# Attention scores as three passes of split operands, one sum untied, last products in halves

## The chip, the cores and the metric

The kernel runs on one core of a Trainium2 chip. The core has a matrix engine (TensorE, PE in the profile, with PEld for its weight loads), a vector engine (VectorE, DVE), a scalar engine (ScalarE, ACT), a general engine (GpSimd, POOL) and a queue engine that issues transfers (SyncE, SP). Each works through its own instructions in order; semaphores tie them together. The metric is the device time of one execution in microseconds. The kernel before takes 1212.84 us, the median of three runs from 1212.77 to 1212.94.

## The reference

A trunk of two layers over one sequence of 256 tokens with 1024 features, all float32. Each layer is a half-step feed-forward block, a mixer and another half-step feed-forward block, each followed by a layer norm of `alpha * x + h`:

```python
for l in range(DEPTH):
    h = _swiglu(x, ffn_w1[l, 0], ffn_w3[l, 0], ffn_w2[l, 0])
    x = _layernorm(ALPHA * x + 0.5 * h, ln_g[l, 0], ln_b[l, 0])
    h = _mixer(x, l, w_in[l], ...)
    x = _layernorm(ALPHA * x + h, ln_g[l, 1], ln_b[l, 1])
    h = _swiglu(x, ffn_w1[l, 1], ffn_w3[l, 1], ffn_w2[l, 1])
    x = _layernorm(ALPHA * x + 0.5 * h, ln_g[l, 2], ln_b[l, 2])
```

The mixer projects x to seven parts: u and v for a gating unit with causal mixing of positions, q, k and values for attention, and two gates. The attention has 8 heads, and each head has two halves of 64 dimensions with a softmax of their own:

```python
q, k = _rope(q, cos, sin), _rope(k, cos, sin)
s = jnp.einsum('bqhmd,bkhmd->bhmqk', q_blk, k) * scale     # m: the two halves of a head
p = jax.nn.softmax(jnp.where(mask, s, neg), axis=-1)
a = p[:, :, 0] - lam * p[:, :, 1]
o = jnp.einsum('bhqk,bkhe->bqhe', a, v)
```

Queries are taken in blocks of 128, so the first block sees 128 keys and the second 256.

## The kernel before, in words

**Split operands.** The large products are made from float32 values that are split in two: a high part, rounded to the type F32R by a copy on ACT, and a low part, the difference, by a subtraction on DVE. A product is then three multiplies of F32R: high by high, high by low, low by high. `split` (L232) does this for activations, `stream` (L155) for weights: a transfer into `raw`, a copy on ACT (L174) to `whi`, a subtraction on DVE (L178) to `wlo`. `three` (L268) issues the three multiplies for row-wise products; `gemm_a2` (L273) does column-wise products for two blocks of 128 output features, with 16 multiplies of 512 columns from the high weights (L283) and 16 of 256 from the low weights (L290).

**Order.** TensorE's instructions run in the order in which the program issues them. For the other engines a planner chooses the order from priorities; `soon()` raises the priority, and `behind(ins)` places an instruction after `ins` in its engine's order. Work that belongs beside the weight products, such as attention, is written as generators: `beside(task, delay)` starts one after a delay, and each `yield w` lets `w` units pass. Time for them is counted in `beat`s of the issued products; one call of `gemm_a2` for one weight block is two units. So delays decide where in TensorE's order a task's multiplies stand.

**Attention.** For each of four pairs of heads, `rope` (L795) makes q and then k with `gemm_a2`, exchanges rows by four transfers on SyncE's queue (L801), multiplies by the cosine on DVE (L804) and the sine on GpSimd (L805), and `rest` adds the two (L809), 1.55 units later (1.25 for the last). It returns one float32 tile of 128 rows by 512 columns: the rows are the two halves `m` of a head, 64 each, and the columns are two heads `j` of 256 tokens. `attend` (L815) starts 3.9 units after k. `exps(1)` (256 keys) and, 0.6 units later, `exps(0)` (128 keys) each issue four score calls at L829, for two heads and two halves, plain float32, 64 rows high, into one bank of TensorE's accumulators (PSUM) per half. DVE then adds the mask and takes the row extreme (L837), ACT takes the exponentials (L839), DVE combines the halves (L848), TensorE transposes (L863, L868), ACT copies (L865, L870), TensorE multiplies by the values (L876, L878), and ACT copies and squares that sum (L881, L886). The banks for this come from four `side` banks in turn; the four `main` banks serve the projections.

**Norms.** Each norm adds bank sums to the residual rows, for two blocks of 128 rows (t) and two halves of 512 columns (c): `part_s` (L542) on DVE, with a row sum. `finish_s` (L548) makes the mean (L551), squares on ACT (L553), an inverse root by short DVE steps, and the normalised rows (L556). Then `turn` (L622) brings the rows into the transposed layout, by TensorE transposes (L633) or transfers, and splits them (L233, L234) for the next stage. `xlo[0, 0]` is the subtraction that ends the first of these for t = 0. In the mixer `done` (L996) issues both sums of a row block at the end of its products, after the first rows' `turn`; in the feed-forward block the sums are issued half by half (L767).

**The end.** The last norm works with `part` (L562): a sum, statistics by groups of 256 columns and, for the last rows, a product with the gain (L574), which the finish (L576) uses: TensorE forms parts of the result from it (L588, L592) while DVE computes the inverse root. For the last rows and columns 512 to 1023 the loop at L761 issues 24 multiplies of 512 columns into one bank and then handles two halves of 256.

Of the kernel before, what the change touches and what calls it, by code (L numbers as in the profile page):

```python
# [11 lines left out]
F32 = mybir.dt.float32  # L12
# [8 lines left out]
P = 128  # L21
D = 1024
T = 256
# [35 lines left out]
def trunk(ctx, tc, x, xT, w13a, w13b, w2s, w2p, wb, wqk, wa, wbr, wo, gateb, sgug, sgub, sguwT, sgubias, lam, diffg,  # L59
# [91 lines left out]
    def behind(ins):  # L151

        return tc.issue_after(ins) if ins is not None else nullcontext()
# [355 lines left out]
    class Norm:  # L509
# [31 lines left out]

        def part_s(self, t, c, ps, scale=1.0):  # L542
            y = self.y[t][:, c * 512 : (c + 1) * 512]
            with behind(self.xlo.get((0, 0))):
                V.scalar_tensor_tensor(out=y, in0=y, scalar=scale, in1=ps, op0=ALU.mult, op1=ALU.add,
                                       accum_out=self.st[t][:, c : c + 1])

# [103 lines left out]
    def ffn(l, f, i, norm, following=None):  # L651
# [108 lines left out]
            ln.pre = ahead(following)  # L760
        for t in range(NT):  # L761
            for c in range(2):
                for ps, o, n in ends[t, c]:
                    for q in PQ[-HELD:]:
                        rows_p(ps, t, q, held[q, c], hh, hl, o, n, stop=q == PQ[-1])
                    if not last:
                        ln.part_s(t, c, ps)  # L767
                        continue
                    for o in ((0, 256) if last and (t, c) == (1, 1) else (0,)):
                        ln.part(t, c * 512 + o, ps[:, o : o + 256] if o or last and (t, c) == (1, 1) else ps, 1.0)  # L770
            (ln.finish if last else ln.finish_s)(t, ((2, 1.5), (2, 1))[t])
            if t == 0:
                with behind(ln.ends[0]):
                    ln.more(1, 0, S[7], ALU.subtract, ln.scale)
                    ln.more(1, 0, u, ALU.add)
                    ln.more(1, 1, v, ALU.add, ln.scale)
                    ln.more(1, 1, S[7], ALU.add)
        return ln.close()

    def mixer(l, i, norm):  # L780
# [14 lines left out]
        def rope(src, scale, last=False):  # L795

            (_, z), = gemm_a2([src], both, lambda m: slots("z", 2)[0], lambda: t512("r"), scale)
            sw, r = t512("swap"), slots("qk", 2)[0]
            for q in range(4):
                o, i = q * 32, (q ^ 1) * 32  # L800
                nc.sync.dma_start(sw[o : o + 32, :], z[i : i + 32, :])  # L801
            r3, z3, s3 = (v.rearrange("p (j t) -> p j t", j=2) for v in (r, z, sw))
            c, s = (v.unsqueeze(1).to_broadcast([P, 2, T]) for v in (cos_t, sin_t))
            V.tensor_tensor(out=r3, in0=z3, in1=c, op=ALU.mult)  # L804
            turned_by[0] = G.tensor_tensor(out=s3, in0=s3, in1=s, op=ALU.mult).ins  # L805

            def rest():
                with behind(None if last else added[0]):
                    V.tensor_tensor(out=r, in0=r, in1=sw, op=ALU.add)  # L809
                yield 0  # L810

            beside(rest(), 1.25 if last else 1.55)
            return r

        def attend(hp, qT, kT):  # L815
            mx, sums = sm("mx", 8), sm("sums", 8)
            c4 = sm("c", 4)
            rc = sm("rc", 4)

            def rows(z, m, j, o, n):  # L820
                return z[m * HD : (m + 1) * HD, j * T + o : j * T + o + n]

            def exps(t):

                nk = (t + 1) * P
                banks = [side_bank() for _ in range(2)]
                for j in range(2):
                    for m in range(2):
                        PE.matmul(banks[m][:, j * nk : (j + 1) * nk], rows(qT, m, j, t * P, P), rows(kT, m, j, 0, nk),  # L829
                                  start=True, stop=True)  # L830
                pp = []
                for m in range(2):
                    o = m * 4 + t * 2
                    p = s512("pp")[:, : 2 * nk]
                    for j in range(2):
                        s, a = slice(j * nk, (j + 1) * nk), slice(o + j, o + j + 1)
                        V.tensor_tensor_reduce(out=p[:, s], in0=banks[m][:, s], in1=mask[:, T - nk :], scale=-1.0,  # L837
                                               scalar=BIG, op0=ALU.add, op1=ALU.min, accum_out=mx[:, a])
                        A.activation(p[:, s], p[:, s], AF.Exp, bias=mx[:, a], scale=-1.0, accum_out=sums[:, a])  # L839
                    pp.append(p)  # L840
                return pp

            def less(t, pp):

                nk = (t + 1) * P
                for j in range(2):
                    s = slice(j * nk, (j + 1) * nk)
                    V.scalar_tensor_tensor(out=pp[0][:, s], in0=pp[1][:, s], scalar=c4[:, t * 2 + j : t * 2 + j + 1],  # L848
                                            in1=pp[0][:, s], op0=ALU.mult, op1=ALU.add)
                return pp[0]  # L850

            second = exps(1)
            yield 0.6
            first = exps(0)
            V.reciprocal(out=rc, in_=sums[:, 4:])
            V.scalar_tensor_tensor(out=c4, in0=rc, scalar=neg_lam[l], in1=sums[:, :4], op0=ALU.mult, op1=ALU.mult)
            second, first = less(1, second), less(0, first)
            yield 2.6
            b = side_bank()
            for j in range(2):  # L860
                for c in range(2):
                    o = (j * 2 + c) * P
                    PE.transpose(b[:, o : o + P], second[:, o : o + P], ident)  # L863
            aT1 = slots("aT", 2)[0]
            A.activation(aT1, b, AF.Copy)  # L865
            b = side_bank()
            for j in range(2):
                PE.transpose(b[:, j * P : (j + 1) * P], first[:, j * P : (j + 1) * P], ident)  # L868
            aT0 = slots("aT", 2)[0][:, :T]
            A.activation(aT0, b[:, :T], AF.Copy)  # L870
            yield 2.3
            b = side_bank()
            for j in range(2):
                h = hp * 2 + j
                v = [val[c][:, h // 4, (h % 4) * P : (h % 4 + 1) * P] for c in range(2)]
                PE.matmul(b[:, j * P : (j + 1) * P], aT0[:, j * P : (j + 1) * P], v[0], start=True, stop=True)  # L876
                for c in range(2):
                    PE.matmul(b[:, T + j * P : T + (j + 1) * P], aT1[:, (j * 2 + c) * P : (j * 2 + c + 1) * P],  # L878
                               v[c], start=c == 0, stop=c == 1)
            on = slots("on", 2)[0]  # L880
            A.activation(on, b, AF.Copy)  # L881
            ss, s2 = sm("ss", 4), sm("s2", 4)
            A.activation(s2, sums[:, :4], AF.Square, scale=(2 * HD * EPS) ** 0.5)
            for q in range(4):
                s = slice(q * P, (q + 1) * P)
                A.activation(b[:, s], b[:, s], AF.Square, accum_out=ss[:, q : q + 1])  # L886
            yield 2
            with behind(turned_by[0]):
                G.tensor_tensor(out=ss, in0=s2, in1=ss, op=ALU.add)
            r = rsqrt4(ss, 1.0 / (2 * HD))  # L890
            yield 2
            both_ = tmp.tile([P, 2, 512], F32, tag="columns", name=name("both"), bufs=1)
            os, pk = both_[:, 0], both_[:, 1].bitcast(U16)
            for q in range(4):
                t, j = q // 2, q % 2
                with behind(emptied[0]):
                    A.activation(os[:, j * T + t * P : j * T + (t + 1) * P], on[:, q * P : (q + 1) * P], AF.Copy,
                                 scale=r[:, q : q + 1])
            planes(pk, os)
            tt = turning(pk, 4)  # L900
            yield LAND
            b = slots("turned", 2)[0]
            join(b, tt)
            dl = dgs[:, l : l + 1]
            for j in range(2):
                h, s = hb[hp * 2 + j], slice(j * T, (j + 1) * T)
                A.activation(h[:, :T], b[:, s], AF.Copy, scale=dl)
                V.scalar_tensor_tensor(out=h[:, T:], in0=b[:, s], scalar=dl, in1=h[:, :T].bitcast(F32),
                                        op0=ALU.mult, op1=ALU.subtract)

        for hp in range(HEADS // 2):
            qT = rope(wqk[l, hp, 0], HD ** -0.5)
            kT = rope(wqk[l, hp, 1], 1.0, hp == HEADS // 2 - 1)
            beside(attend(hp, qT, kT), 3.9)

        gates = []
        for br, sec in ((0, GA_), (1, GB_)):
# [183 lines left out]
```

## Time and profile before

| | us |
|---|---|
| median of the runs | 1212.84 |
| lowest, highest | 1212.77, 1212.94 |
| the profiled execution | 1213.05 |
| its span | 1211.3 |
| TensorE busy | 1203.7 (99%) |
| VectorE busy | 942.9 (78%) |
| ScalarE busy | 857.4 (71%) |
| GpSimd busy | 91.1 (8%) |

The span runs from the first to the last profiled instruction; the device time has 1.75 us around it. Names like L829 are lines of the kernel. In a timeline a row is a start, a length and a group of like instructions, with their count after the x; several rows may overlap, since multiplies are pipelined and their ends are modelled. In brackets stands how long the engine was idle before the row and whose work ended that. A row of windows gives, for one stretch, its length and then the busy time and count of TensorE, its weight loads, VectorE, ScalarE and GpSimd, the granted clock, the share of the transfer engines and GB/s. A row of groups gives the count, the total and the mean time (ns) and the idle time before.

### The profile page before, as it was taken

The numbers are of one execution on the slowest core, as the hardware profiler recorded it, in microseconds if no ns is written. First come the engines' busy times: TensorE is split into PE (matmuls) and PEld (weight loads), VectorE is DVE, ScalarE is ACT, GpSimd is POOL, SyncE is SP. The second block draws the span as 40 slices with busy tenths as digits, with TensorE's granted clock in tenths as the row PEclk, the third lists the DMA queues.
The fourth block names the chain that finished last, engine by engine and source line by source line (L and its number), as shares of the span: only waits on it lengthen the run. The fifth ranks groups of instructions, "written<-read, shape, count | busy, mean of one in ns | idle before, by whom it ended". The sixth has DMA issues, their size and how long they took to land.

```text
span 1211.3 us, 16542 instructions
## 1 busy us (share of the span) xinstructions
PE 1203.7 (99%) x5961; PEld 1011.3 (83%) x5961; DVE 942.9 (78%) x1540; ACT 857.4 (71%) x1384; POOL 91.1 (8%) x184
## 2 busy tenths in 40 slices
PE   9999999999999999999999999999999999999998
PEld 8888888888888878888888888888888888888886
DVE  6658998885696876579985679989766877757797
ACT  7677677679865595776776776776898556867761
POOL 0100000233300000000000000003331000000000
PEclk9999999999999999999999999999999999999999
DMA  8985665655764658665668665766648456677551
GB/s 321 323 261 174 211 249 208 227 177 166 232 227 164 217 178 282 191 192 218 229 216 270 195 176 207 254 223 199 213 139 273 176 174 217 201 259 210 184 202 47
DMA packets 101346, 257.00 MB, mean 212 GB/s; under 512 B 66528, under 2 KB 67600, under 8 KB 74640
## 3 DMA queue, kind: packets, MB, share of 16 engines
q1 hardware_dynamic: 97296, 243.03, 59.9%
q0 software_dynamic: 3536, 12.13, 3.2%
q8 instruction: 46, 0.75, 0.3%
q10 hardware_dynamic: 432, 0.79, 0.2%
q14 instruction: 36, 0.29, 0.1%
HBM read 235.47 MB, written 1.05 MB: 195 GB/s over the span
## 4 chain that ended last, share of the span: by engine, by line
PE 91%; DVE 4%; ACT 3%; issue 1%; DMA 0%; SPq 0%; POOL 0%; DVEq 0%; ACTq 0%; POOLq 0%
PE bank L271 35%; PE sbank L271 24%; PE bank L283 16%; PE bank L290 8%; PE sbank L283 2%; PE bank L446 2%; PE sbank L290 1%; PE sbank L829 1%; DVE wlo L178 1%; PE sbank L961 1%; ACT pp L839 0%; DVE nwa L248 0%; ACT xf L638 0%; ACT whi L174 0%; PE sbank L878 0%
## 5 line engine op out<-in xcount | busy, mean ns | idle before, releaser
L178 DVE TENSOR_TENSOR wlo<-raw,whi 128x1024 fp32r<-128x1024 f32 (+1 forms) x396 | 436.6, 1125 | 144.5 <-ACT whi L174 113.9
L174 ACT ACTIVATE whi<-raw 128x1024 fp32r<-128x1024 f32 (+1 forms) x396 | 372.9, 971 | 124.4 <-PE bank L283 43.2
L271 PE MATMUL bank<-whi,x 128*128 128x512 f32 x840 | 263.3, 390 | 0.0
L271 PEld LDWEIGHTS bank<-whi,x 128*128 128x128 f32 x840 | 157.7, 188 | 32.9 <-DVE gz L293 0.2
L271 PE MATMUL bank<-wlo,x 128*128 128x512 f32 x420 | 163.5, 389 | 0.0
L271 PE MATMUL sbank<-whi,x 128*128 128x512 f32 x512 | 158.9, 389 | 0.0
L283 PE MATMUL bank<-x,whi 128*128 128x512 f32 x640 | 156.0, 394 | 0.0
L283 PEld LDWEIGHTS bank<-x,whi 128*128 128x128 f32 x640 | 117.1, 188 | 26.3 <-issue 2.3
L271 PEld LDWEIGHTS sbank<-whi,x 128*128 128x128 f32 x512 | 96.1, 188 | 20.0
L353 ACT ACTIVATE shi<-raw 128x1024 fp32r<-128x1024 f32 (+1 forms) x80 | 73.4, 946 | 51.7 <-DVE raw L368 26.4
L271 PE MATMUL sbank<-wlo,x 128*128 128x512 f32 x256 | 99.6, 389 | 0.0
L355 DVE TENSOR_TENSOR slo<-raw,shi 128x1024 fp32r<-128x1024 f32 (+1 forms) x80 | 85.4, 1088 | 14.1 <-ACT shi L353 13.3
L271 PEld LDWEIGHTS bank<-wlo,x 128*128 128x128 f32 x420 | 78.9, 188 | 16.0
L290 PE MATMUL bank<-x,wlo 128*128 128x256 f32 x640 | 85.9, 285 | 0.0
L290 PEld LDWEIGHTS bank<-x,wlo 128*128 128x128 f32 x640 | 81.6, 191 | 2.2
L291 ACT ACTIVATE r<-bank 128x256 f32<-128x256 f32 x112 | 41.6, 377 | 24.0 <-PE bank L290 24.0
L271 PEld LDWEIGHTS sbank<-wlo,x 128*128 128x128 f32 x256 | 48.1, 188 | 9.9
L271 PE MATMUL sbank<-whi,hhi 128*128 128x512 f32 x144 | 56.3, 391 | 0.0
L271 PE MATMUL sbank<-whi,hlo 128*128 128x512 f32 x144 | 56.1, 390 | 0.0
L271 PE MATMUL sbank<-wlo,hhi 128*128 128x512 f32 x144 | 56.0, 389 | 0.0
L506 POOL DMA_DIRECT2D bc<-in_lng x6 | 3.2, 530 | 696.2 <-DVE bc L505 696.2
L702 ACT ACTIVATE planes<-silu 128x1024 uint16<-128x1024 uint16 x40 | 42.0, 1053 | 7.3 <-DVE silu L701 6.2
(247 smaller groups left out, 1999.1 us busy)
## 6 DMA issues: line engine op xcount, KB each, us to landing
raw<-in_w13b SPq DMA_DIRECT2D x76, 1024.0 KB, 5.4
raw<-in_w2p SPq DMA_DIRECT2D x24, 1024.0 KB, 4.9
raw<-in_wa SPq DMA_DIRECT2D x24, 1024.0 KB, 5.4
raw<-in_w2s SPq DMA_DIRECT2D x20, 1024.0 KB, 4.9
raw<-in_wb SPq DMA_DIRECT2D x16, 1024.0 KB, 5.3
raw<-in_wqk SPq DMA_DIRECT2D x16, 1024.0 KB, 4.8
raw<-in_wbr SPq DMA_DIRECT2D x16, 1024.0 KB, 4.9
raw<-in_w13a SPq DMA_DIRECT2D x8, 1024.0 KB, 4.8
```

The costliest lines, as they stand in the source:

```text
L174: copied = A.activation(h, r, AF.Copy)
L178: V.tensor_tensor(out=w, in0=r, in1=h.bitcast(F32), op=ALU.subtract)
L271: PE.matmul(ps, xx, w, start=start and n == 0, stop=stop and n == 2)
L283: PE.matmul(b[-1], hi[:, k * P : (k + 1) * P], xc(k), start=k == 0, stop=False)
L290: PE.matmul(b[n][:, :T], lo[:, k * P : (k + 1) * P], xc(k)[:, :T], start=False, stop=k == KT - 1)
L291: emptied[0] = A.activation(r[:, s], b[n][:, T:], AF.Copy, scale=scale).ins
L353: A.activation(h, r, AF.Copy)
L355: V.tensor_tensor(out=w, in0=r, in1=h.bitcast(F32), op=ALU.subtract)
L446: PE.matmul(ps[t][m], x[:, j, o + t * P : o + (t + 1) * P], y, start=k0 + j == 0 and o == 0 and y is hi, stop=k0 + j == KT - 1 and y is lo)
L702: A.activation(pk.rearrange("p (w k) -> p w k", w=2), s.bitcast(U16).rearrange("p (k w) -> p w k", w=2), AF.Copy)
L829: PE.matmul(banks[m][:, j * nk : (j + 1) * nk], rows(qT, m, j, t * P, P), rows(kT, m, j, 0, nk), start=True, stop=True)
L961: PE.matmul(b[:, j * T + t * P : j * T + (t + 1) * P], vg[t][:, g // 4, s], wsT[g // 4][:, s], start=True, stop=True)
```

## The change

Three edits.

1. `rope` now returns two F32R tiles: a copy of the sum r on ACT, issued with raised priority, and 0.5 units later a subtraction on DVE for the low part. The score calls become three per head and half, (q high, k high), (q high, k low), (q low, k high), which add up in the same bank; the loop over the two halves is innermost. `attend` starts 4.4 units after k in place of 3.9. Each rope takes two more tiles of the pool.
2. `part_s` places only the second half's sum (c = 1) behind `xlo[0, 0]`; the first half's sum has no such place.
3. For the last rows and the last 512 columns, the multiplies are issued as 24 of 256 columns into the left half of the old bank and 24 into a new bank. The left half is finished (sum, statistics, product with the gain) when its multiplies are done, and what the old bank's right half holds from earlier products is added to the rows by one more DVE sum.

```diff
         def part_s(self, t, c, ps, scale=1.0):
             y = self.y[t][:, c * 512 : (c + 1) * 512]
-            with behind(self.xlo.get((0, 0))):
+            with behind(self.xlo.get((0, 0)) if c else None):
                 V.scalar_tensor_tensor(out=y, in0=y, scalar=scale, in1=ps, op0=ALU.mult, op1=ALU.add,
                                        accum_out=self.st[t][:, c : c + 1])
...
         for t in range(NT):
             for c in range(2):
-                for ps, o, n in ends[t, c]:
-                    for q in PQ[-HELD:]:
-                        rows_p(ps, t, q, held[q, c], hh, hl, o, n, stop=q == PQ[-1])
-                    if not last:
-                        ln.part_s(t, c, ps)
-                        continue
-                    for o in ((0, 256) if last and (t, c) == (1, 1) else (0,)):
-                        ln.part(t, c * 512 + o, ps[:, o : o + 256] if o or last and (t, c) == (1, 1) else ps, 1.0)
+                (ps, _, _), = ends[t, c]
+                if last and (t, c) == (1, 1):
+                    y, right = ln.y[t][:, 768:], bank()
+                    for b, o, opens in ((ps, 0, False), (right, 256, True)):
+                        for q in PQ[-HELD:]:
+                            rows_p(b[:, :T], t, q, held[q, c], hh, hl, o, 256, stop=q == PQ[-1],
+                                   start=opens and q == PQ[-HELD])
+                        ln.part(t, 512 + o, b[:, :T], 1.0)
+                        if not opens:
+                            V.tensor_tensor(out=y, in0=y, in1=ps[:, T:], op=ALU.add)
+                    continue
+                for q in PQ[-HELD:]:
+                    rows_p(ps, t, q, held[q, c], hh, hl, 0, 512, stop=q == PQ[-1])
+                if last:
+                    ln.part(t, c * 512, ps, 1.0)
+                else:
+                    ln.part_s(t, c, ps)
...
-            sw, r = t512("swap"), slots("qk", 2)[0]
+            sw, r, hi = t512("swap"), slots("qk", 2)[0], slots("qkh", 4, F32R)
...
             def rest():
                 with behind(None if last else added[0]):
                     V.tensor_tensor(out=r, in0=r, in1=sw, op=ALU.add)
-                yield 0
+                with soon():
+                    A.activation(hi[0], r, AF.Copy)
+                yield 0.5
+                with behind(None if last else added[0]):
+                    V.tensor_tensor(out=hi[1], in0=r, in1=hi[0].bitcast(F32), op=ALU.subtract)
 
             beside(rest(), 1.25 if last else 1.55)
-            return r
+            return hi
...
                 for j in range(2):
-                    for m in range(2):
-                        PE.matmul(banks[m][:, j * nk : (j + 1) * nk], rows(qT, m, j, t * P, P), rows(kT, m, j, 0, nk),
-                                  start=True, stop=True)
+                    for n, (q, k) in enumerate(((0, 0), (0, 1), (1, 0))):
+                        for m in range(2):
+                            PE.matmul(banks[m][:, j * nk : (j + 1) * nk], rows(qT[q], m, j, t * P, P),
+                                      rows(kT[k], m, j, 0, nk), start=n == 0, stop=n == 2)
...
-            beside(attend(hp, qT, kT), 3.9)
+            beside(attend(hp, qT, kT), 4.4)
```

## The prediction

> **What bounds the kernel now.** I read the page first: busy times, then the chain that ended last.
>
> ```profile
> span 1211.3 us, 16542 instructions
> PE 1203.7 (99%) x5961; PEld 1011.3 (83%) x5961; DVE 942.9 (78%) x1540; ACT 857.4 (71%) x1384; POOL 91.1 (8%) x184
> PEclk9999999999999999999999999999999999999999
> PE 91%; DVE 4%; ACT 3%; issue 1%; DMA 0%; SPq 0%; POOL 0%; DVEq 0%; ACTq 0%; POOLq 0%
> L290 PEld LDWEIGHTS bank<-x,wlo 128*128 128x128 f32 x640 | 81.6, 191 | 2.2
> ```
>
> TensorE is busy 99% of the span at full clock and carries 91% of the chain. The loads of the low weights, L290, wait for no producer worth naming: weights are split long before use. A microsecond counts, then, only if it is taken out of TensorE's own stream, out of a place where that stream stands, or out of the tail. The chain of waits in order of time gives the steps of that stream, and timelines of single stretches give the rest.
>
> ```profile
> 209.16 1.91 PE bank L290 x16
> 211.08 3.65 PE bank L283 x16
> ...
> 27.70 21.76 PE sbank L271 x96
> ```
>
> A split multiply of 512 columns steps by 21.76/96 = 0.227 us, one of 256 columns by 1.91/16 = 0.119 us.
>
> **Edit 1: the scores.** Timelines of TensorE: one head pair of the second layer, the last head pair of the first layer, and transposes.
>
> ```profile
> 841.34 1.13 PE L829 MATMUL sbank<-qk,qk 64*128 64x256 f32 x8
> 842.40 2.14 PE L283 MATMUL bank<-x,whi 128*128 128x512 f32 x8
> 844.47 0.72 PE L829 MATMUL sbank<-qk,qk 64*128 64x128 f32 x8
> 845.11 1.19 PE L283 MATMUL bank<-x,whi 128*128 128x512 f32 x4
> ...
> 272.22 1.94 PE L829 MATMUL sbank<-qk,qk 64*128 64x256 f32 x8
> 274.08 0.96 PE L283 MATMUL bank<-x,whi 128*128 128x512 f32 x3
> ...
> 273.02 0.73 PEld L829 LDWEIGHTS sbank<-qk,qk 64*128 64x128 f32 x6 [0.51 <-ACT sbank L886]
> ...
> 269.57 0.60 PE L863 MATMUL sbank<-ident,pp 128*128 128x128 f32 x4
> 270.00 0.38 PE L868 MATMUL sbank<-ident,pp 128*128 128x128 f32 x2
> ```
>
> Each head pair has two blocks: 256 keys, 842.40 - 841.34 = 1.06 us, and 128 keys, 845.11 - 844.47 = 0.64 us. A block is four calls and shows eight records, so a plain f32 call is two records. Eight records in 0.64 us are 0.08 us each, while one full-height multiply of 128 columns steps by 0.43/4 = 0.1075 us (the transposes). So the two 64-row halves run side by side: a block is four slots of two records. The blocks differ by 0.42 us over four slots: 0.105 us per slot and 128 columns. What stays, 1.06 - 8 x 0.105 = 0.22 us, is the block's entry and exit.
>
> After the change each call is three split calls, each one record, halves alternating: six slots per block. With 256 keys a slot is between 0.105 (half of the present 0.21) and 0.119 (L290); I take the middle, 0.112: 0.22 + 6 x 0.112 = 0.89, a gain of 0.17. With 128 keys no row shows a split multiply. Below: half of today's slot, 0.0525, makes 0.535, a gain of 0.10. Above: twice today's slot, 0.21, makes 1.48, a loss of 0.84. The nearest row is the transpose, one record, same columns, same weight load: 0.1075, so 0.22 + 0.645 = 0.865, a loss of 0.225. Together +0.055 us per head pair, **+0.4 us** over eight (ends -2.5 and +5.7). Six slots replace four: where a load of 128 columns sets the pace, halving the passes gains nothing.
>
> The Trainium skill, page "TensorE: Matmul & The Clock Gate", section LDWEIGHTS, speaks against this edit: a load's time goes with its columns, not its rows, some 107 ns for 128; its section on weight-path modes adds that the fast load is not for FP32. By that rule the short block comes out as taken above, and the transpose step of 0.1075 us agrees. The page "FP8 and Floating Point Precision", section TensorE Precision Notes, counts true FP32 as four passes; three for four by columns alone would shorten both blocks, the first rival below.
>
> The split itself adds one ACT copy and one DVE subtraction of 128x512 per rope, 16 of each (groups of the page and of the view by line, a window over six ropes, and two rows of DVE in it):
>
> ```profile
> L178 DVE TENSOR_TENSOR wlo<-raw,whi 128x1024 fp32r<-128x1024 f32 (+1 forms) x396 | 436.6, 1125 | 144.5 <-ACT whi L174 113.9
> L174 ACT ACTIVATE whi<-raw 128x1024 fp32r<-128x1024 f32 (+1 forms) x396 | 372.9, 971 | 124.4 <-PE bank L283 43.2
> ...
> L233 ACT ACTIVATE hhi<-columns 128x512 fp32r<-128x512 f32 x20 | 12.5, 623 | 0.0
> L234 DVE TENSOR_TENSOR hlo<-columns,hhi 128x512 fp32r<-128x512 f32 x20 | 13.8, 689 | 3.5 <-ACT hhi L233 3.1
> ...
> 227.00:272.00 45.00, 45.00 (x288) 38.06 (x287) 38.29 (x102) 34.31 (x100) 13.24 (x21) 1.00 0.59 199
> ...
> 268.78 0.61 DVE L848 SCALAR_TENSOR_TENSOR pp<-pp,c,pp 128x128 f32<-128x128 f32 x2
> 269.31 0.68 DVE L809 TENSOR_TENSOR qk<-qk,swap 128x512 f32<-128x512 f32 x1
> ```
>
> In that window DVE is busy 38.3 of 45 us and ACT 34.3; six ropes add 6 x 0.69 = 4.1 to the one, 94%, and 6 x 0.62 = 3.7 to the other, 85%. Neither becomes the bound, and the weights keep their lead; that is the cover. Behind the copy on ACT stand exponentials and weight copies, behind the subtraction on DVE the lows and row sums. The tight places are the attention's own steps. In the first layer the last pair's block stood 0.51 us for a bank that ACT L886 still read, and the break in alternation cost more: 1.86 against 1.06. One copy of 0.62 us ahead of L886 makes that 0.6 longer. Transposes at 270.00 follow their input (269.39) by 0.6 us, and a copy and a subtraction (1.31) could eat that: I take 0.2 in each layer. **+1.0 us** in all; below, -0.8 (the half unit by which attention moves lets the bank come free), above the fourth rival. The half unit itself costs TensorE nothing: the same multiplies are dealt out later, with the projections filling in.
>
> **Edit 2: the sum at the mixers' norms.** Timeline around the first mixer's end, and the transposes that waited:
>
> ```profile
> 423.39 0.69 DVE L178 TENSOR_TENSOR wlo<-raw,whi 128x512 fp32r<-128x512 f32 x1
> ...
> 426.12 0.69 DVE L234 TENSOR_TENSOR x<-xf,x 128x512 fp32r<-128x512 f32 x1 [2.05 <-ACT x L233]
> 426.73 0.68 DVE L545 SCALAR_TENSOR_TENSOR xtok<-xtok,bank 128x512 f32<-128x512 f32 x1
> 427.52 0.63 ACT L174 ACTIVATE whi<-raw 128x512 fp32r<-128x512 f32 x1
> 428.04 0.63 ACT L233 ACTIVATE x<-xf 128x512 fp32r<-128x512 f32 x1
> 428.06 0.21 DVE L551 TENSOR_SCALAR mv<-st 128x1 f32<-128x1 f32 x1
> 428.56 1.14 ACT L553 ACTIVATE sq<-xtok,mv 128x1024 bf16<-128x1024 f32 x1
> ...
> 425.90 0.39 PE L271 MATMUL bank<-whi,mlo 128*128 128x512 f32 x1
> ...
> 433.11 0.39 PE L271 MATMUL bank<-whi,x 128*128 128x512 f32 x1
> 433.89 0.66 PE L633 MATMUL sbank<-ident,xtok 128*128 128x128 f32 x4 [0.39 <-DVE xtok L556]
> ```
>
> DVE stands 2.05 us before L234. The first bank's last multiply is 12 before the one at 425.90, at 423.18, so its sum fits in the idle time, and the second sum and the mean come 0.6 us earlier (the sum's place at 426.73 is free). The goal would be the transposes' stand, 433.89 - 433.11 - 0.227 = 0.55 us, once per mixer. But the squares (L553) start when ACT has finished L233, not when the mean is there: 428.06 + 0.21 = 428.27 against 428.56. A mean at 427.67 finds ACT just begun on L174 (427.52), and only another order on ACT turns it into time. **0** taken, nearest to that row; ends -1.1 (both stands gone) and 0: the idle 2.05 us excludes a loss. At the feed-forward norms nothing is tied yet when the first sum of the second rows is issued, so nothing moves.
>
> **Edit 3: the last products.** Timeline of the end:
>
> ```profile
> 1197.48 0.39 PE L271 MATMUL sbank<-whi,hhi 128*128 128x512 f32 x1
> ...
> 1200.05 0.69 DVE L574 TENSOR_TENSOR xtok<-xtok,bc 128x512 f32<-128x512 f32 x1
> ...
> 1202.69 0.40 PE L271 MATMUL sbank<-whi,hlo 128*128 128x512 f32 x1
> 1203.13 0.75 DVE L567 TENSOR_TENSOR xtok<-xtok,sbank 128x256 f32<-128x256 f32 x2 [2.38 <-PE sbank L271]
> 1204.46 0.41 DVE L574 TENSOR_TENSOR xtok<-xtok,bc 128x256 f32<-128x256 f32 x1
> 1204.78 0.26 DVE L579 BATCH_NORM_AGGREGATE mv<-st 128x2 f32<-128x24 f32 x1
> ```
>
> Now 24 multiplies of 512 from 1197.48, the sum 0.44 after the last start, and 1.65 us of two sums, two statistics and a product until the aggregate. Then 48 of 256: the last starts at 1197.48 + 47 x 0.119 = 1203.07, its sum 0.44 - 0.108 later (the shorter multiply), 1203.40, which is 0.27 late; but only one sum and one statistic are left, 0.42 each with 0.04 behind: aggregate at 1204.32, **-0.45 us**, and everything after it waits for it in order. The left half's four operations (the added sum among them, 1.84 us) start at 1200.74, when L574 is done, and end at 1202.6: hidden by the right half's multiplies with 0.8 to spare; uncovered, the added sum costs 0.42. Ends: -0.7 (step 0.1135, half of 0.227) and 0.
>
> **Sum:** 0.4 + 1.0 + 0 - 0.45 = +0.95. The profiled execution took 1213.05 us for its span of 1211.3, 0.2 above the median 1212.84, so 1214.0 for it and **1213.8** for the median.
>
> **Rivals.** (a) *Columns set the pace, not loads.* Slots 0.105 and 0.0525: -0.21 and -0.105 per pair, x 8 = -2.5; with -0.45 and no new waits 1209.9. For it: halves load at the same time today. Against: no record of 128 columns steps under 0.105. (b) *Short split multiplies run at a quarter rate*, slots 0.21: (0.84 - 0.17) x 8 = +5.4, with 0.55 from the rest 1218.8. For: the kernel has no split multiply under 256 columns. Against: nothing in the trace slows with fewer columns. (c) *Halves do not overlap in split form*: 12 steps, 1.65 and 1.51 us, +1.46 x 8 = 11.7: 1225.1. Against: the f32 halves overlap, and their order alternates. (d) *The split comes late.* The last k was summed at 269.99, its block began at 272.22: 2.2 us; half a unit (1.4 us, a rope of 5.57 us being two units) makes 3.6. Copy, subtraction, one ACT weight copy and one DVE low ahead of them (0.62 + 0.69 + 0.97 + 1.13 = 3.4) use it up. From a second weight copy on, TensorE stands 1.0 at each of the four later pairs: +4.2 with 0.4 - 0.45 gives 1217.0. (e) *Edit 2 does nothing*, because ACT keeps its order: that is the forecast.
>
> **Chances.** Forecast 0.53 with its own range 1212.0 to 1215.8; (a) 0.18; (b) 0.10; (c) 0.05; (d) 0.14. The range 1210.0 to 1218.0 leaves out (c), most of (b) and the outer side of (a). Within 0.2% (2.4 us) is what I call no change: faster 0.16 ((a) but for its inner edge, and a little of the forecast), slower 0.30 ((b), (c), (d)), same 0.54.
>
> **What would show it.** Blocks of L829's successor at 0.89 and 0.865 us with 12 records in six slots: step right; 0.535 for the short one: (a); above 1.4: (b) or, with starts not in pairs, (c). Waits of score loads for the subtraction: (d). The squares still starting behind L233: edit 2 as forecast. The aggregate 1.25 us behind the last multiply's start: edit 3. Wrong would be a total outside 1212.0 to 1215.8, or within it by cancelling errors.

## The result

The changed kernel takes 1226.43 us (median of 4 runs, 1225.79 to 1227.10), the kernel before 1212.80 us on the same chip (1212.56 to 1212.94). The ratio is 1.0114, with a 95% interval of 1.0101 to 1.0126. That is 13.6 us slower, outside the predicted range of 1210 to 1218. The profiled execution took 1225.79 us.

From the page of the changed kernel: span, TensorE's and the other engines' busy time, and the shares of the chain that ended last.

```profile
span 1224.1 us, 16754 instructions
PE 1208.5 (99%) x6049; PEld 1018.0 (83%) x6049; DVE 950.6 (78%) x1557; ACT 864.9 (71%) x1400; POOL 85.8 (7%) x184
...
PE 87%; DVE 5%; ACT 3%; DMA 1%; POOL 1%; issue 1%; SPq 1%; DVEq 0%; POOLq 0%; ACTq 0%
```

TensorE is busy 4.8 us more, in a span that is 12.8 us longer: it now stands for 15.6 us instead of 7.6. POOL, SP's queue and the DMA, which had 0% of the chain, have 1% each. A landmark tells where: the transposes that wait at the second rows of each mixer's norm, before (first row, the second layer; the first layer's stands in the prediction, at 433.89) and after.

```profile
1032.84 0.55 PE L633 MATMUL sbank<-ident,xtok 128*128 128x128 f32 x3 [0.38 <-DVE xtok L556]
```

```profile
439.69 0.66 PE L633 MATMUL sbank<-ident,xtok 128*128 128x128 f32 x4 [0.29 <-DVE xtok L556]
...
1046.01 0.66 PE L633 MATMUL sbank<-ident,xtok 128*128 128x128 f32 x4 [0.33 <-DVE xtok L556]
```

The first layer loses 439.69 - 433.89 = 5.8 us, the second 1046.01 - 1032.84 - 5.8 = 7.4, and the rest gains 13.2 - 12.8 = 0.4. TensorE's timeline of the changed kernel shows an ordinary head pair, and the last head pair of each layer:

```profile
229.63 0.97 PE L843 MATMUL sbank<-qkh,qkh 64*128 64x256 f32 x12
230.53 2.14 PE L283 MATMUL bank<-x,whi 128*128 128x512 f32 x8
232.60 0.89 PE L843 MATMUL sbank<-qkh,qkh 64*128 64x128 f32 x12
233.41 0.86 PE L290 MATMUL bank<-x,wlo 128*128 128x256 f32 x5
...
274.45 0.38 PE L843 MATMUL sbank<-qkh,qkh 64*128 64x256 f32 x1
279.11 1.65 PE L843 MATMUL sbank<-qkh,qkh 64*128 64x256 f32 x11 [4.28 <-ACT aT L879]
...
884.42 1.65 PE L843 MATMUL sbank<-qkh,qkh 64*128 64x256 f32 x11 [4.19 <-ACT aT L879]
886.00 3.78 PE L283 MATMUL bank<-x,whi 128*128 128x512 f32 x8
```

The score blocks themselves are near the forecast: 230.53 - 229.63 = 0.90 us and 233.41 - 232.60 = 0.81 us. But in the last pair of each layer the second half of the first block stands 4.28 and 4.19 us for a side bank from which ACT has not yet copied the transposes of the pair before. Behind it the clock falls: eight multiplies that take 2.14 us in the ordinary pair (230.53) take 3.78. By stages of the changed kernel (the columns end with the granted clock, the DMA share and GB/s):

```profile
272.00:281.00 9.00, 4.72 (x28) 3.67 (x26) 3.67 (x8) 8.46 (x24) 0.43 (x2) 0.90 0.56 157
281.00:284.00 3.00, 3.00 (x16) 2.16 (x15) 1.05 (x8) 3.00 (x11) 1.93 (x10) 0.74 0.84 317
877.00:884.00 7.00, 3.23 (x19) 2.40 (x17) 2.52 (x5) 6.14 (x14) 0.74 (x2) 0.95 0.62 183
884.00:891.00 7.00, 6.58 (x33) 5.06 (x34) 2.71 (x10) 6.53 (x22) 3.07 (x15) 0.56 0.48 155
```

Length of the stage times the missing share of the clock is what the clock costs: 9 x 0.10 + 3 x 0.26 = 1.7 us in the first layer and 7 x 0.05 + 7 x 0.44 = 3.4 in the second. With the stands that is 6.0 and 7.6, against 5.8 and 7.4 lost. So two stands, and the clock behind them, account for the loss, to 0.2 us in each layer.

Why the bank is late is read backwards. First ACT in the changed kernel, ahead of that copy:

```profile
260.34 0.63 ACT L820 ACTIVATE qkh<-qk 128x512 fp32r<-128x512 f32 x1 [2.94 <-DVE qk L818]
...
272.54 0.99 ACT L911 ACTIVATE both<-on,nwy 128x128 f32<-128x128 f32 x3 [3.57 <-POOL nwy L264]
...
278.00 0.58 ACT L895 ACTIVATE on<-sbank 128x512 f32<-128x512 f32 x1
278.47 0.58 ACT L879 ACTIVATE aT<-sbank 128x512 f32<-128x512 f32 x1
```

ACT stands 3.57 us in front of the scaling of the first pair's output (L911), and the copy (L879) is some 6 us behind it in the same queue. The scaling waits for the inverse root of the first pair, which is on GpSimd. GpSimd's timeline before, and after:

```profile
259.69 0.20 POOL L889 TENSOR_TENSOR ss<-s,ss 128x4 f32<-128x4 f32 x1
...
265.44 0.20 POOL L264 TENSOR_TENSOR nwy<-nwa,nwy 128x4 f32<-128x4 f32 x1
265.62 1.30 POOL L805 TENSOR_TENSOR swap<-swap,sin_t 128x512 f32<-128x512 f32 x1
```

```profile
264.20 1.30 POOL L814 TENSOR_TENSOR swap<-swap,sin_t 128x512 f32<-128x512 f32 x1 [4.62 <-DMA swap<-z]
265.47 0.19 POOL L903 TENSOR_TENSOR ss<-s,ss 128x4 f32<-128x4 f32 x1
...
270.91 1.32 POOL L263 TENSOR_SCALAR nwa<-nwa 128x4 f32<-128x4 f32 x1
272.31 0.20 POOL L264 TENSOR_TENSOR nwy<-nwa,nwy 128x4 f32<-128x4 f32 x1
```

Before, the root ran from 259.69 to 265.64, ahead of the eighth rope multiply. After, the half unit by which attention starts later has put the root behind that multiply, and the multiply waits 4.62 us for the exchange of the last k's rows by DMA. The root ends at 272.51: 6.9 us later, of which 5.8 are its later start and 1.1 its own greater length.

### The profile page after: what moved, and what is told of

Same layout as the page of the kernel before. It is cut to its first block, busy times and chain, and to the rows that moved or that the text cites. A ratio compares the mean times of both kernels' runs of the same rounds, so it can differ in the third digit from the quotient of the medians.

```text
span 1224.1 us, 16754 instructions
## 1 busy us (share of the span) xinstructions
PE 1208.5 (99%) x6049; PEld 1018.0 (83%) x6049; DVE 950.6 (78%) x1557; ACT 864.9 (71%) x1400; POOL 85.8 (7%) x184
## 4 chain that ended last, share of the span: by engine, by line
PE 87%; DVE 5%; ACT 3%; DMA 1%; POOL 1%; issue 1%; SPq 1%; DVEq 0%; POOLq 0%; ACTq 0%
PE bank L271 35%; PE sbank L271 23%; PE bank L283 14%; PE bank L290 8%; PE sbank L283 2%; PE bank L446 2%; PE sbank L290 1%; DMA swap<-z 1%; DVE wlo L178 1%; SPq L810 1%; PE sbank L843 1%; ACT whi L174 1%; PE sbank L975 1%; DVE nwa L248 0%; POOL swap L814 0%
## 5 line engine op out<-in xcount | busy, mean ns | idle before, releaser
L178 DVE TENSOR_TENSOR wlo<-raw,whi 128x1024 fp32r<-128x1024 f32 (+1 forms) x396 | 434.9, 1120 | 170.5 <-ACT whi L174 138.8
L283 PE MATMUL bank<-x,whi 128*128 128x512 f32 x640 | 160.4, 400 | 0.0
L271 PE MATMUL sbank<-whi,hhi 128*128 128x512 f32 (+1 forms) x144 | 55.5, 386 | 0.0
L271 PE MATMUL sbank<-whi,hlo 128*128 128x512 f32 (+1 forms) x144 | 55.3, 384 | 0.0
L271 PE MATMUL sbank<-wlo,hhi 128*128 128x512 f32 (+1 forms) x144 | 55.2, 384 | 0.0
```

Source lines behind the costliest of these rows:

```text
L178: V.tensor_tensor(out=w, in0=r, in1=h.bitcast(F32), op=ALU.subtract)
L271: PE.matmul(ps, xx, w, start=start and n == 0, stop=stop and n == 2)
L283: PE.matmul(b[-1], hi[:, k * P : (k + 1) * P], xc(k), start=k == 0, stop=False)
```

## The experiments

Two theories stood at the start. *Order*: the later start puts the first pair's root behind the eighth rope multiply on GpSimd, and that makes the bank late. *Queues*: the copy and the subtraction, standing ahead of other work in the in-order queues of ACT and DVE, make it late. Some expectations call these A and B.

**late_only**: the kernel before with the later start alone.

```
-            beside(attend(hp, qT, kT), 3.9)
+            beside(attend(hp, qT, kT), 4.4)
```

> The kernel before with one number changed: attention starts 4.4 units after k in place of 3.9; scores stay plain f32, nothing is split. Theory A (order): the later start alone puts the first pair's inverse root on GpSimd behind the last rope's multiply, ACT stands for it, and the last pair's score block waits over 4 us for a bank in each layer: 1219 to 1227, the first eight inverse-root steps on GpSimd only after the eighth rope multiply. Theory B (split work): the copies on ACT and subtractions on DVE make the queues late; without them 1212 to 1214.

Measured: 1218.46 us (1216.75 to 1219.41), ratio 1.0046 (1.0031 to 1.0061). Timelines of late_only:

```profile
276.25 1.13 PE L829 MATMUL sbank<-qk,qk 64*128 64x256 f32 x6 [1.83 <-ACT aT L865]
...
261.08 1.54 POOL L805 TENSOR_TENSOR swap<-swap,sin_t 128x512 f32<-128x512 f32 x1 [1.79 <-DMA swap<-z]
...
269.68 0.70 ACT L897 ACTIVATE both<-on,nwy 128x128 f32<-128x128 f32 x2 [4.35 <-POOL nwy L264]
```

The same stand at the same bank, without any split, by the same path; it is shorter, 1.83 us for 4.28, and here the eighth multiply starts at 261.08, not 264.20. The later start alone costs 5.8 us (the kernel before took 1212.70 in the same rounds), a little under half of the loss.

**split_early**: the changed kernel with the start as before.

```
-            beside(attend(hp, qT, kT), 4.4)
+            beside(attend(hp, qT, kT), 3.9)
```

> The changed kernel with attention started 3.9 units after k as before; split, sum and last products as changed. Theory A: GpSimd's order is that of before, so no wait of 4 us; what is left is the split's own cost of 0 to 2 us: 1211.5 to 1214.5. Theory B: the copies and subtractions are all there and have less time, so at least as slow as the changed kernel: 1225 or more.

Measured: 1226.37 us (1225.42 to 1227.79), 1.0114 (1.0098 to 1.0129): no gain, so order alone is not the answer. Timelines of split_early, GpSimd, DVE and TensorE:

```profile
263.01 1.30 POOL L814 TENSOR_TENSOR swap<-swap,sin_t 128x512 f32<-128x512 f32 x1 [12.75 <-DMA swap<-z]
269.42 1.28 POOL L814 TENSOR_TENSOR swap<-swap,sin_t 128x512 f32<-128x512 f32 x1
...
270.74 0.69 DVE L818 TENSOR_TENSOR qk<-qk,swap 128x512 f32<-128x512 f32 x1 [3.66 <-POOL swap L814]
...
273.36 0.84 PE L877 MATMUL sbank<-ident,pp 128*128 128x128 f32 x4 [2.84 <-DVE pp L862]
```

Here the root is ahead of the eighth multiply again, as before the change. But the seventh multiply, behind which the root stands, starts at 263.01 and not at 258.43 as before the change, so root and eighth multiply are late, and with them the last k's sum on DVE; the third pair's weighted differences (L862) stand behind that sum, and the transposes wait for them. In addition the waits of TensorE show 1.5 us for k's low half (L823) in four blocks.

**tail_as_before**: the changed kernel with an earlier place for the transposes, so that the steps behind them fall where they fell before.

```
-            yield 2.6
+            yield 2.1
```

> The changed kernel with the transposes' delay 2.1 in place of 2.6 units, so that all of attention behind the scores is issued where it was before, while the scores start later. Theory A: 1211.5 to 1214.5, with the inverse root of the first pair between the seventh and the eighth rope multiply on GpSimd. Theory B: 1224 to 1227, the last pair's block held by 4 us or more.

Measured: 1216.13 us (1215.38 to 1217.12), 1.0030 (1.0019 to 1.0041). On GpSimd the root stands ahead of the eighth multiply. The first blocks of pairs 2 and 3 still run 0.55, 0.58, 0.55 and 0.79 us over 0.90, for a side bank. Three quarters of the loss is gone, and neither theory had this number.

**sum_and_halves**: edits 2 and 3 alone; the diff is that of the change without its attention hunks.

> Only the untied sum and the last products in halves, scores as before. Prediction: the aggregate of the last norm 0.45 us earlier, the squares of the mixers' norms where they were: 1212.2 to 1212.5. If the squares do move and the transposes no longer stand, 1211.2 to 1211.8.

Measured: 1212.23 us (1212.02 to 1212.79), 0.9996 (0.9987 to 1.0006), as expected: no measurable difference.

**root_early**: the changed kernel, with the root half a unit earlier and the rest where it was.

```
             for q in range(4):
                 s = slice(q * P, (q + 1) * P)
                 A.activation(b[:, s], b[:, s], AF.Square, accum_out=ss[:, q : q + 1])
-            yield 2
+            yield 1.3
             with behind(turned_by[0]):
                 G.tensor_tensor(out=ss, in0=s2, in1=ss, op=ALU.add)
             r = rsqrt4(ss, 1.0 / (2 * HD))
-            yield 2
+            yield 2.7
```

> The changed kernel with one step of the attention moved: the yield ahead of a head pair's inverse root is 1.3 instead of 2, the next one 2.7 instead of 2. TensorE's order of work stays that of the changed kernel; on GpSimd the first pair's inverse root goes back ahead of the eighth rope multiply, as before the change. Theory order (the eighth rope multiply ahead of the first root on GpSimd is what makes scaling, aT copies and so the bank late): last pairs' S1 blocks lose their 4.2 us stands, the clock stays near 1 behind them, 1214 to 1218 us. Theory queues (the copy and the subtraction, standing ahead of other work in the in-order queues of ACT and DVE, are what makes it late, whatever GpSimd's order): the stands stay above 2 us, 1221 to 1227 us.

Measured: 1220.95 us (1220.57 to 1221.57), 1.0066 (1.0051 to 1.0081). TensorE's instructions and their order are the changed kernel's; what moves is the root on GpSimd, back ahead of the eighth multiply, and the time falls by 5.5 us. The root is not the only thing that moves: behind it ACT and DVE have another order too (ACT's L895 is at 272.52, ahead of two weight copies, where the changed kernel has it at 278.00 behind them). So the 5.5 us belong to the root's place together with the order that follows from it. The time lies between what the two theories gave. The rest is again a stand at the last pairs' first blocks, but for another reader of a bank. Timeline of root_early:

```profile
880.03 1.19 PE L843 MATMUL sbank<-qkh,qkh 64*128 64x256 f32 x11 [2.29 <-ACT sbank L900]
881.16 3.43 PE L283 MATMUL bank<-x,whi 128*128 128x512 f32 x8
```

Now it is the bank of the last products, held until ACT has done four squares (L900) between weight copies.

**nosoon**: the changed kernel without the raised priority of the copy.

```
-                with soon():
-                    A.activation(hi[0], r, AF.Copy)
+                A.activation(hi[0], r, AF.Copy)
```

> The changed kernel without the raised priority of the copy on ACT: the copy of a rope's high half then stands in ACT's queue where its issue puts it. GpSimd's order is that of the changed kernel. Theory order: no gain, 1224 to 1228 us, with stands near 4 us at the last pairs' S1 blocks. Theory queues, in the form that the copy standing 2.9 us ahead of the first pair's aT copies makes those late: the stands fall below 2.5 us, as in late_only, and the time to 1217 to 1221 us.

Measured: 1226.09 us (1225.25 to 1226.76), 1.0107 (1.0090 to 1.0124). But the edit moved nothing: ACT's instructions come in the same order as in the changed kernel, and the stand ahead of the copy (260.34 above) is still there. Timeline of nosoon:

```profile
260.47 0.63 ACT L819 ACTIVATE qkh<-qk 128x512 fp32r<-128x512 f32 x1 [2.93 <-DVE qk L818]
```

So this run says nothing for or against the queues.

**keep_nosoon**: both of the above, the transposes' place of tail_as_before and no raised priority.

> The changed kernel with the yield ahead of the transposes 2.1 instead of 2.6 (as tail_as_before, 1216.1 us) and without the raised priority of the copy on ACT; GpSimd's order is that of before the change. Theory order: the same as tail_as_before, 1215.5 to 1217 us. Theory queues: another gain, 1213 to 1215 us. Should the score loads then wait for a late high half, 1217 to 1221 us, with waits for ACT's copy at the S1 blocks.

Measured: 1216.08 us (1215.69 to 1216.85), 1.0028 (1.0017 to 1.0039), the same as tail_as_before. Here too ACT's order is that of the run without the edit, so this is tail_as_before once more and no test.

**copies_unused** and **a39_copies_unused**: copies and subtractions made, scores in f32 from the unsplit q and k; the start at 4.4 and at 3.9.

```
-                    for n, (q, k) in enumerate(((0, 0), (0, 1), (1, 0))):
-                        for m in range(2):
-                            PE.matmul(banks[m][:, j * nk : (j + 1) * nk], rows(qT[q], m, j, t * P, P),
-                                      rows(kT[k], m, j, 0, nk), start=n == 0, stop=n == 2)
+                    for m in range(2):
+                        PE.matmul(banks[m][:, j * nk : (j + 1) * nk], rows(qT[2], m, j, t * P, P),
+                                  rows(kT[2], m, j, 0, nk), start=True, stop=True)
```

> The changed kernel, with its start of the attention and its copies and subtractions, but the scores computed in f32 from the unsplit q and k, in the form of before: the split parts are made and not used. Against late_only (the same start, no copies) it prices the copies alone, against the changed kernel the scores that need them. Theory order: the copies add little, 1217.5 to 1220 us. Theory queues: they carry the rest, 1223 to 1227 us. If the score multiplies' need for the low half is what matters, it is as low as late_only, 1218.5 us, with the changed kernel 8 us above.

> split_early (the changed kernel with the attention's start at 3.9 as before, 1226.4 us) with the scores computed in f32 from the unsplit q and k, in the form of before; the split parts are made and not used. Theory queues (the copies and subtractions in the in-order queues of ACT and DVE are the loss, whatever the scores read): 1222 to 1228 us, with DVE standing over 3 us for the eighth GpSimd multiply and the transposes behind it. Theory late half (the scores' wait for k's low half is the loss, and what follows from it): 1212 to 1215 us, as sum_and_halves (1212.2) with nothing but hidden copies.

Measured: 1228.08 us (1225.17 to 1230.93), 1.0124 (1.0105 to 1.0143), with the later start: the copies bring late_only's 1218.46 to this, though nothing reads them; the changed kernel is no higher. But the stands lie elsewhere than in the changed kernel. TensorE waits 2.8 us for ACT's aT copy in this run, less than the 3.7 of late_only and the 8.5 of the changed kernel; 3.4 us are waits for the row extremes on DVE (second block of pair 1) and 2.9 us for a DVE step of the gating unit (L956). So the run shows that the copies alone can cost as much, not that they do it by the same steps.

With the start as before: 1218.93 us (1216.77 to 1220.18), 1.0057 (1.0040 to 1.0074), between what the two theories gave. The last pairs' blocks stand there for ACT's aT copy, as in late_only. The difference to split_early, 7.4 us, goes with scores that need the low half: the seventh multiply on GpSimd starts at 258.68 here.

**root_early_sq, tail_sq, e23_sq**: root_early, tail_as_before and sum_and_halves, with the squares read from the copy in SBUF and written over a dead tile, so that the bank is free after the copy (L895).

```
-                A.activation(b[:, s], b[:, s], AF.Square, accum_out=ss[:, q : q + 1])
+                A.activation(aT1[:, s], on[:, s], AF.Square, accum_out=ss[:, q : q + 1])
```

> root_early with the squares of a head's output read from its copy in SBUF (on) and written over a dead tile, so that the bank of the last products comes free after the copy (ACT L895), not after four squares (ACT L900). In root_early (1220.95 us) the last pairs' S1 blocks stand 2.67 us in each layer for a square that ACT does behind weight copies. Theory bank (what a late attention costs is paid as TensorE standing for a side bank, and the clock behind it): both stands go, 2 x 2.67 and about 1 us of lowered clock, 1214 to 1216.5 us. Theory elsewhere (TensorE only stands there what it would stand later): another wait takes their place, 1218.5 to 1221.5 us.

> tail_as_before (the changed kernel with the yield ahead of the transposes 2.1 instead of 2.6, 1216.1 us) with the squares read from the copy, as in root_early_sq. There the S1 blocks of pairs 2 and 3 run 0.55, 0.58, 0.55 and 0.79 us over, named for ACT's squares once in each layer and for ACT's aT copy once. Theory bank: the squares' share goes, 1214.5 to 1215.6 us; all of it, 1213.6 us, if the aT copies, which stand behind the squares, come earlier too. Theory elsewhere: 1215.8 to 1217 us.

> sum_and_halves (the sum untied and the last products in halves, scores as before, 1212.2 us) with the squares read from the copy. Its last pair's block in the first layer runs 0.32 us over, and no other does. Theory bank: 1211.5 to 1212.2 us, within 0.2% of before. Anything above 1213.5 would say that moving the squares off the bank has a cost of its own, and would have to be taken off the two runs above.

Measured: root_early_sq 1214.53 us (1214.18 to 1215.87), 1.0016 (1.0007 to 1.0026), 6.4 below root_early. tail_sq 1213.57 us (1213.19 to 1214.51), 1.0007 (0.9998 to 1.0016): no measurable difference to before. e23_sq 1211.77 us (1211.40 to 1213.70), 0.9995 (0.9986 to 1.0004). Where the bank comes free in time, most of the loss does not come back at a later place. In root_early_sq ACT still stands ahead of the copy of a high half, as in the changed kernel:

```profile
260.22 0.64 ACT L820 ACTIVATE qkh<-qk 128x512 fp32r<-128x512 f32 x1 [3.22 <-DVE qk L818]
```

So that stand alone is not the loss, which nosoon could not show. Timeline of tail_sq, last pair of the second layer:

```profile
875.03 0.97 PE L843 MATMUL sbank<-qkh,qkh 64*128 64x256 f32 x12
875.93 2.14 PE L283 MATMUL bank<-x,whi 128*128 128x512 f32 x8
877.99 0.89 PE L843 MATMUL sbank<-qkh,qkh 64*128 64x128 f32 x12
878.81 0.39 PE L290 MATMUL bank<-x,wlo 128*128 128x256 f32 x1
```

0.90 and 0.82 us, where the changed kernel stood. So with the transposes half a unit earlier and the squares off the bank, the change has no stand at the score blocks, and its time is that of before within the interval. No kernel here is faster than before by more than 0.2%.

## Why the prediction was wrong, by its steps

**The step that failed** is in edit 1: "The half unit itself costs TensorE nothing: the same multiplies are dealt out later, with the projections filling in", and with it the waits of +1.0 us. I had counted the multiplies that move and not the other work that is dealt out by the same clock: the aT copies, the squares, and the root on GpSimd, which passed from ahead of the eighth rope multiply to behind it. late_only measures this step by itself: +5.8 us, not 0. In the changed kernel the stands and the clock behind them take 6.0 and 7.6 us, where the sum has +1.0 for both layers together. I had even entered the later start as a possible gain ("lets the bank come free"); its sign was wrong.

**The cover for the copies.** I argued from busy shares: DVE at 94% and ACT at 85% leave room. The sum of work did fit: DVE was busy 41.55 of the 45 us of that window, 92%, and TensorE all of it. What the later start leaves of the loss is 8.0 us (1226.43 - 1218.46), and it goes with the split, for edits 2 and 3 alone cost nothing (sum_and_halves). From traces alone, a path for it is this. DVE's drains of the last k's bank, in the changed kernel and in late_only:

```profile
255.47 0.69 DVE L823 TENSOR_TENSOR qkh<-qk,qkh 128x512 fp32r<-128x512 f32 x1
256.07 2.36 DVE L178 TENSOR_TENSOR wlo<-raw,whi 128x1024 fp32r<-128x1024 f32 x2
258.34 0.76 DVE L293 TENSOR_TENSOR z<-bank,r 128x256 f32<-128x256 f32 x2
```

```profile
256.27 0.75 DVE L293 TENSOR_TENSOR z<-bank,r 128x256 f32<-128x256 f32 x2
```

In the changed kernel the subtraction and two lows stand ahead of the drain, which is 2.1 us later. Its rows go through the exchange by DMA to the eighth multiply, 3.1 us later (264.20 against 261.08), and the stand is 2.4 us longer. Over both layers the stands are 4.8 us longer (4.28 and 4.19 for 1.83 and 1.87), and the clock costs 3.4 us more than in late_only, which loses 1.7 us in the second layer and nothing in the first: 8.2 in all, for the 8.0. The last 1.0 of the 3.1 us the drain does not explain. No run moved that drain by itself, so this link is read and not tested, and why the copies cost 8 us in the changed kernel stays open. copies_unused has the same time with the copies unused, but by other stands.

**The score blocks** held: 0.90 and 0.81 us for 0.89 and 0.865 forecast, 12 records in six slots, the halves in pairs (only the second block of pair 1 runs 0.25 us over in each layer). Where nothing stands the cost is +0.01 us per pair and not +0.055. Rivals (a), (b) and (c) fall by these rows; that the 1225.1 us of (c) are near the measured time is chance.

**Rival (d)**, the split coming late, named a wait that the changed kernel hardly has; with the earlier start it is there, 1.5 us in four blocks of split_early, and the scores' need for the low half accounts for 7.4 us of that kernel. The half unit in the change is what avoids it, and it is paid for on GpSimd. I priced each of the two without the other. (In its price, four stands of 1.0 us are 4.0, not the 4.2 of the sum.)

**Edit 2** came out as forecast at about nothing, but not for the reason I gave. Timelines of sum_and_halves, ACT, DVE and TensorE:

```profile
427.38 0.62 ACT L174 ACTIVATE whi<-raw 128x512 fp32r<-128x512 f32 x1
427.90 1.14 ACT L553 ACTIVATE sq<-xtok,mv 128x1024 bf16<-128x1024 f32 x1
...
429.73 0.68 DVE L234 TENSOR_TENSOR x<-xf,x 128x512 fp32r<-128x512 f32 x1
...
433.70 0.66 PE L633 MATMUL sbank<-ident,xtok 128*128 128x128 f32 x4 [0.34 <-DVE xtok L556]
```

ACT did change its order: the squares start 0.66 us earlier (427.90 for 428.56), ahead of L233. Then DVE puts the low part L234, which used to stand ahead of the root, between the root's steps (429.73), and the transposes are 0.19 us earlier (433.70 for 433.89). Of the 0.66 and the 0.19, 0.14 us are there already at the weight copy ahead (427.38 for 427.52), and the transposes' stand is 0.34 us for 0.39. The step "squares behind L233" was wrong; that the value came out nearly right is luck.

**Edit 3** held in size and mechanism. The end of the changed kernel:

```profile
1216.27 0.28 PE L271 MATMUL bank<-whi,hlo 128*128 128x256 f32 x1
...
1216.59 0.42 DVE L567 TENSOR_TENSOR xtok<-xtok,bank 128x256 f32<-128x256 f32 x1 [1.33 <-PE bank L271]
...
1217.51 0.26 DVE L579 BATCH_NORM_AGGREGATE mv<-st 128x2 f32<-128x24 f32 x1
```

The aggregate is 1.24 us behind the last multiply's start, for 1.25 forecast, and the stretch behind the second layer is 0.4 us shorter, for 0.45.

The sum comes close for a change without its stands: tail_sq, which is the change plus two moved steps, takes 1213.57 us, for 1213.8 forecast. That is in part luck, from terms that cancel: its scores cost +0.1 instead of +0.4, its waits at the score blocks are zero instead of +1.0, and it has others, of 1.4 us in all, for ACT's L233 behind two of the norms.

## What to carry to other kernels

When a change moves the start of a group of work by a fixed step, list everything that is dealt out by the same clock, on every engine and queue, and ask of each small operation what it passes; here a chain of fifteen tiny GpSimd operations fell behind one DMA-fed multiply, and putting it back ahead, with the order that followed, was worth 5.5 us. A share of 85 or 94% says that added work fits, not that the instruction behind it can wait: follow each added instruction to the next one in its queue that feeds TensorE's banks. Release a bank by the first copy, not by a later reader that stands in a busy queue.

## What the runs showed of the hardware

**A stand can be paid twice.** In the changed kernel the clock's loss of 1.7 us behind the first stand and 3.4 behind the second (worked out above), at half rate, makes 3.4 and 6.8 us of halved clock. A stand need not be as long as 4.2 us for it. In root_early both layers stand for the squares, 2.3 us each by its waits; in the first layer TensorE goes on at 277.39, in the second at 880.03. By stages of root_early, one that takes in the first stand and 3.6 us behind it, and three behind the second:

```profile
272.00:281.00 9.00, 6.71 (x49) 5.08 (x47) 6.19 (x16) 9.00 (x26) 2.82 (x10) 1.00 0.72 197
...
881.00:882.00 1.00, 1.00 (x5) 0.75 (x3) 1.00 (x6) 1.00 (x3) 0.67 (x5) 0.50 1.21 225
883.00:884.00 1.00, 1.00 (x4) 0.78 (x3) 0.00 (x0) 1.00 (x5) 0.67 (x5) 0.50 0.97 385
884.00:885.00 1.00, 1.00 (x11) 0.63 (x11) 0.00 (x0) 1.00 (x5) 0.75 (x4) 0.99 1.05 434
```

In the first layer the clock stays at 1.00, in the second it is halved until about 884. In late_only a stand of 1.87 us in the second layer did it too (0.62, 0.50, 0.50 and 0.68 in the four stages of 1 us from 879), and one of 1.83 us in the first did not (1.00). The Trainium skill, page "TensorE: Matmul & The Clock Gate", section "What's actually happening", has a free-running activity window of about 3.4 us and a half-rate clock after an idle one. The half rate, and stretches of 3.4 us and twice that, agree with the rows; that 2.29 and 1.87 us were enough does not agree with a window that has to be idle throughout, and here the measurement decides.

**Small GpSimd operations end with DVE's subtractions.** The root's step L263 took 1.32 us at 270.91 in the changed kernel; its median over 24 is 0.22. DVE in the same stretch:

```profile
270.93 1.21 DVE L178 TENSOR_TENSOR wlo<-raw,whi 128x1024 fp32r<-128x1024 f32 x1
```

The step ends at 272.23, just behind DVE's subtraction (272.14). In the changed kernel ten of the root's small steps take over 0.7 us; in each of them such a subtraction (L178) was running, and each ends 0.06 to 0.09 us behind it. The Trainium skill, page "SBUF — State Buffer", section "SBUF: two separate sides", describes a port pair that a DVE operation with two SBUF inputs and a GpSimd operation take in turns, each for its whole length; this agrees, but for this step's start 0.02 us ahead of the subtraction. No run took DVE's work away from that stretch.
